# Zeroing both layers' gate arrays in the first mixer, with a fourth activation buffer and a third kept group

## The chip, the core and the metric

One core of a Trainium2 chip runs the whole kernel. The metric is the device time of one execution in microseconds, the median of several runs. The engines named below are TensorE (PE, its weight loads PEld), VectorE (DVE), ScalarE (ACT), GpSimd (POOL) and SyncE (SP, which only issues transfers). SP, ACT and POOL each have a queue on which they issue DMA transfers.

## The reference

A decoder trunk of two layers on 512 tokens of width 1024, in float32. Each layer has a token mixer and a channel mixer, each followed by a layer norm of `alpha * h + sublayer(h)`.

```
for layer in range(2):
    mix = mixer_ab(h, ...) if layer == 0 else mixer_c(h, ...)
    h = layer_norm(alpha * h + mix)
    h = layer_norm(alpha * h + peer(h, ...))
```

The channel mixer (PEER) has 16384 experts. For each token, eight heads each find 16 experts by a two-part key search, with softmax weights called gates:

```
s_top, i_top = top_k(einsum('thpd,hpkd->thpk', q, sub_keys), 16)
cand = s_top[:, :, 0, :, None] + s_top[:, :, 1, None, :]
best, pos = top_k(cand.reshape(T, 8, 256), 16)
gate = softmax(best)
act = gelu(einsum('td,thkd->thk', x, u_tab[eid]))
out = einsum('thk,thkd->td', gate * act, v_tab[eid])
```

## The kernel before

The kernel treats the expert layer as dense matrix products for most tokens: the activations `gelu(x @ u^T)` of all 16384 experts are made, multiplied by a mostly empty array of gates and then by `v`. The experts come in 128 blocks of 128, four blocks to a group, 32 groups. Every fp32 operand is cut into a high part (a cast on ACT, line 173) and a low part (a subtraction on DVE, line 174), and each product is three matmuls (`mm3`, lines 189 to 191; `mm2`, line 1155).

The tokens are split three ways. Tokens 64 to 383 go the dense way entirely. The first 64 have their activations made by gathering rows of `u` (`urow`, line 752) and are then added to a gate array in DRAM, after which their `v` side is dense as well. The last 128 are gathered on both sides (`gather_rounds`, line 1001).

A layer passes through three stages.

- **Mixer.** `mixer_ab` in layer 0, `mixer_c` in layer 1, then the output projection and the norm. Weights stream in pieces of 512 KB through the five buffers of `raw` (`stream`) on SP's queue. In `mixer_ab` the four projections run in the order u (`pool_part`), q and k, v, g; `sums` (line 478 and after) works on u and is called after the q and k projection.
- **Routing.** `peer` opens a pool and makes a `Scatter` object. Its constructor creates the DRAM array `gz` of the layer (32 groups x 128 x 512 values, 8.4 MB), fills a tile with zeros on POOL (line 79) and writes it 32 times to DRAM, once for each group, on SP's queue (line 81). Then the key search runs, and beside it `lookahead` makes the activations of the first 24 groups (`NLA`): four blocks at a time into a tile `ge`, of which there are three. A finished tile is spilled to DRAM (`sp`, line 775) unless its group is one of the last two (`KEEP`), which stay on chip. The gathered activations of the first 64 tokens are added into `gz` by indirect transfers on POOL (line 131). The gates of the other dense tokens are built on chip and stored to a second DRAM array, `gd` (line 947); for the three groups that come first afterwards they are also copied into tiles (`self.first`).
- **Experts.** `experts` walks over all 32 groups in the list `order`: one fresh group (number 27), the kept ones, then the fresh ones spread evenly among the spilled. For each group `fetch` gets the activations (a spilled group is loaded again on ACT's queue, line 1060; a fresh one is computed) and the gates: `gd` (line 1066) and `gz` (line 142), on ACT's queue after the first few, into one of three `gt` tiles. `high` and `low` multiply and split (lines 1100, 1104, 1111), `mm2` accumulates. Between the blocks, `gather_rounds` handles the last 128 tokens.

The program text gives dependencies, not the order of issue: the framework arranges each engine's instructions in advance, by a simulation in which an instruction can be issued as soon as it is ready. `issue_after` pins an instruction behind another on one engine. Within an engine's queue the order is then fixed.

The pool `sm` holds the small tiles of the norms (statistics, deviation and its reciprocal), four of each. Tiles called `gap` are never used; they take up space. The statistics of a block's first half (line 284) are taken as soon as the first half of the output projection is there.

Of the kernel before, what the change touches and what calls it, by code (L numbers as in the profile page):

```python
# [9 lines left out]
F32 = mybir.dt.float32  # L10
# [10 lines left out]
P = 128  # L21
# [8 lines left out]
NB = 4  # L30
NG = NE // NB
TD = 3 * P
NU = 64
TN = TD - NU
# [5 lines left out]
NSD = TD // 32  # L40
NLA = 24
NSZ = 4
KEEP = 2
ROT = 3
RAW = 5
QS = 8
# [16 lines left out]
class Scatter:  # L63


    def __init__(self, k, pool, layer):
        nc, self.tc = k.nc, k.tc
        self.name = "gz%d" % layer
        self.layer = layer
        self.head, self.last, self.now = -1, [], []  # L70
        self.todo = []
        self.rows = []
        self.gate = [k.pe.tile([P, 2, 16], F32, name="gate0", tag="gate0", bufs=4) for _ in range(4)]
        self.idx = [k.pe.tile([P, 2 * 16], I32, name="idx0", tag="idx0", bufs=4) for _ in range(4)]
        self.pcol = pool.tile([P, 1], F32, name="pcol", tag="pcol")
        nc.sync.dma_start(out=self.pcol, in_=k.io["pcol"])
        self.dst = k.dram.tile([NG, P, NSZ, NB, 32], F32, name=self.name, tag=self.name)
        z = pool.tile([P, NSZ * NB * 32], F32, name="zero", tag="zero")
        nc.gpsimd.memset(z, 0.0)
        for g in range(NG):  # L80
            nc.sync.dma_start(out=self.dst[g].rearrange("p s b t -> p (s b t)"), in_=z)

    def place(self, k, pool, c, k0, k1):
        nc = k.nc
# [62 lines left out]
class Kern:  # L147
    def __init__(self, ctx, tc, io):
        self.tc = tc
        self.nc = tc.nc  # L150
        self.io = io
        self.dmaq = 0
        E = ctx.enter_context
        self.const = E(tc.tile_pool(name="const", bufs=1))
        self.big = E(tc.tile_pool(name="big", bufs=1))
        self.st = E(tc.tile_pool(name="st", bufs=6))
        self.raw = E(tc.tile_pool(name="raw", bufs=RAW))
        self.sm = E(tc.tile_pool(name="sm", bufs=4))
        self.dram = E(tc.tile_pool(name="dram", bufs=1, space=DRAM))
        self.psA = E(tc.tile_pool(name="psA", bufs=2, space=PSUM))  # L160
        self.psB = E(tc.tile_pool(name="psB", bufs=3, space=PSUM))
        self.psC = E(tc.tile_pool(name="psC", bufs=3, space=PSUM))
# [145 lines left out]
    def mixer_ab(self, xT, hs):  # L308
        nc, tc, io = self.nc, self.tc, self.io
        with tc.tile_pool(name="ab", bufs=1) as ab, tc.tile_pool(name="abk", bufs=1) as abk:  # L310
# [39 lines left out]
                    rot.extend([r1, r2])  # L350

            self.proj_T(w, 1, xT, sink_qk)
            for n in range(4):
                sums(n)
            q1, q2, k1, k2 = rot
            qd = []
            for i, q in enumerate((q1, q2)):
                t = ab.tile([P, T], F32, name="qd%d" % i, tag="qk%d" % i)
# [32 lines left out]
            for h in range(4):  # L391
                s = ab.tile([P, NTB, P], F32, name="sc%d" % h, tag="t%d" % h)
# [6 lines left out]
            for tb in range(NTB):  # L399
# [9 lines left out]
                if tb < NTB - 1:  # L409
                    new = []  # L410
                    for i in range(2):
# [3 lines left out]
                        if state is None:  # L415
                            s = ab.tile([P, 512], F32, name="state%d" % i, tag="state%d" % i)
                            nc.vector.tensor_tensor(s, pk, bd, ALU.mult)
                        else:
                            s = state[i]
                            d = ab.tile([P, 512], F32, name="dst", tag="qk%d" % (2 + i))  # L420
# [14 lines left out]
            for tb in range(NTB):  # L435
                for h in range(4):
                    k = tb * 4 + h
# [3 lines left out]
            def turn(tb):  # L441
                self.transpose_in(o[:, tb].rearrange("p h e -> p (h e)"), xT, 4, 4, tb)
# [15 lines left out]
            self.proj_N(w, 3, xT, sink_g)  # L458
            turn(NTB - 1)
        return xT  # L460

    def pool_part(self, ab, xT, ya, w, icnt, pw, psc):
        nc = self.nc
# [231 lines left out]
    def peer(self, layer, xT, hs, out):  # L695
        nc, tc, io = self.nc, self.tc, self.io
        gd = self.dram.tile([NG, P, NSD - NSZ, NB, 32], F32, name="gd%d" % layer, tag="gd%d" % layer)
        sp = self.dram.tile([NLA, P, NB, TN], F32, name="sp%d" % layer, tag="sp%d" % layer)
        with tc.tile_pool(name="pe", bufs=1) as pe:
            self.pe = pe  # L700
            self.eid = pe.tile([P, P], I32, name="eid", tag="eid")
            self.gate3 = pe.tile([P, P], F32, name="gate3", tag="gate3")
            self.x3 = pe.tile([P, D], F32, name="x3", tag="x3")
            g, b = self.load_ln(layer, 0)

            def norm(tb):
                self.layernorm(tb, hs[tb], g, b, xT)
                if tb == NTB - 1:
                    nc.scalar.copy(self.x3, hs[tb])
                    nc.scalar.mul(hs[tb], hs[tb], ALPHA)  # L710

            self.out_proj(io["c_w_out" if layer else "ab_w_out"], xT, hs, norm)
            self.kept = {}
            self.urows = 0
            self.xx = pe.tile([P, D], F32, name="xx", tag="lng")
            for q in range(QN):
                nc.scalar.copy(self.xx[q * NU:(q + 1) * NU], hs[0][:NU])
            look = self.lookahead(layer, xT, sp)
            with tc.tile_pool(name="rk", bufs=1) as rk, ExitStack() as late:
                gz = Scatter(self, rk, layer)  # L720
                kT = rk.tile([P, (TD - P) // GW, 4, GW], F16, name="kT", tag="kT")
                iot = rk.tile([P, P, 2], F16, name="iot", tag="iot")
                nc.gpsimd.iota(iot, pattern=[[1, P], [0, 2]], base=0, channel_multiplier=0,
                               allow_small_or_imprecise_dtypes=True)
                credit = CREDIT0

                def routing():
                    yield from self.route_topk(layer, xT, kT, gz)
                    self.gx = late.enter_context(tc.tile_pool(name="gx", bufs=1))
                    self.first = {g: self.gx.tile([P, NSD, NB, 32], F32, name="gt", tag="gt", bufs=3)  # L730
                                  for g in (NLA + ROT, NLA - 2, NLA - 1)}
                    yield from self.route_gates(layer, kT, iot, gd)

                for cost in routing():
                    credit += cost
                    while credit >= 2.8:
                        credit -= 2.8
                        next(look, None)
                for _ in look:
                    pass  # L740
                g1, b1 = self.load_ln(layer, 1)
                self.experts(layer, xT, hs, gd, gz, sp, lambda tb: self.layernorm(
                    tb, hs[tb], g1, b1, None if layer else xT, out if layer else None))
        return xT
# [21 lines left out]

    def lookahead(self, layer, xT, sp):
        for g in range(NLA):
            ge = self.pe.tile([P, NB, TN], F32, name="ge", tag="ge", bufs=3)
            for b in range(NB):  # L770
                self.mm1(layer, g * NB + b, xT, ge[:, b, :], b % 2 == 1)
                if g >= NLA - KEEP:
                    self.kept[g] = ge
                elif b == NB - 1:
                    self.nc.sync.dma_start(out=sp[g], in_=ge)
                yield
# [252 lines left out]
    def experts(self, layer, xT, hs, gd, gz, sp, norm):  # L1029
        nc, tc, io = self.nc, self.tc, self.io  # L1030
        with tc.tile_pool(name="ex", bufs=2) as ex, tc.tile_pool(name="ga", bufs=2) as ga:
            ex.tile([P, 88], F32, name="gap", tag="gap", bufs=1)
            accs = [[(self.psC if hf else self.psB).tile([P, 512], F32, name="pC" if hf else "pB",
                                                          tag="pC" if hf else "pB") for hf in range(2)]
                    for _ in range(3)]
# [14 lines left out]
            def fetch(n):  # L1050
                if n >= NG:
                    return
                g = order[n]
                if g in kept:
                    ge = self.kept[g]
                else:
                    ge = self.pe.tile([P, NB, TN], F32, name="ge", tag="ge", bufs=3)
                q = nc.scalar if n > 1 else nc.sync
                if g < NLA and g not in kept:
                    q.dma_start(out=ge, in_=sp[g])  # L1060
                if g in self.first:
                    gt = self.first[g]
                    gz.read(nc.gpsimd, gt[:, :NSZ], g)
                else:
                    gt = self.gx.tile([P, NSD, NB, 32], F32, name="gt", tag="gt", bufs=3)
                    q.dma_start(out=gt[:, NSZ:], in_=gd[g])
                    gz.read(q, gt[:, :NSZ], g)
                ges[g] = (ge, gt)
# [49 lines left out]
            for i in range(NE):  # L1118
# [6 lines left out]
                g, b = order[i // NB], i % NB  # L1125
# [15 lines left out]
            for tb in range(3):  # L1141
                for hf in range(2):
                    for b in range(TAIL):
                        self.mm2(accs[tb], tb, cs[b - TAIL], vs[b - TAIL], False, b == TAIL - 1, (hf,))
                    z = hs[tb][:, hf * 512:(hf + 1) * 512]
# [21 lines left out]
    def run(self, out):  # L1167
        nc, io = self.nc, self.io
        self.epst = self.const.tile([P, 1], F32, name="epst", tag="epst")
        self.const.tile([P, 344], F32, name="gap", tag="gap")  # L1170
        nc.vector.memset(self.epst, EPS)
        hs = [self.big.tile([P, D], F32, name="h%d" % tb, tag="h%d" % tb) for tb in range(NTB)]
        xT = self.new_xT()
# [114 lines left out]
```

## Time and profile before

| | us |
|---|---|
| median of 3 runs | 2726.83 |
| lowest and highest | 2723.45, 2726.99 |
| profiled execution, its own time | 2726.43 |
| profiled execution, its span | 2724.6 |

The profile comes from one execution. Busy time is what each engine spent on its instructions; the transfers that an engine issues aren't counted in it. Matmuls overlap each other, so their busy times are an outline of when PE worked, and their number in a stretch tells its pace. "Idle before" is the time an engine stood before an instruction, with what released it; "issue" means that the profile shows nothing that it waited for.

By the timeline, layer 0 has its mixer to about 125 us, routing to about 655, experts to about 1305; layer 1 its mixer to about 1530, routing to about 2065, and experts to the end.

### The profile page before, as it was taken

How to read it: one execution, taken by the hardware profiler on the slowest of the kernel's cores; microseconds unless marked ns; L12 is line 12 of the kernel's file. 1: busy time of each engine (PE TensorE's matmuls, PEld its weight loads, DVE VectorE, ACT ScalarE, POOL GpSimd, SP SyncE). 2: the span in 40 equal slices, each digit the busy share in tenths (PEclk: the TensorE clock that was granted, in tenths of full speed). 3: DMA queues.
4: the chain of work that ended last, by engine and by line, in shares of the span. 5: the costliest groups of instructions: out<-in, count | busy, mean ns of one | idle time of the engine just before them, and what ended most of it. 6: DMA issues, size and time to landing. Idle time of an engine off the chain costs nothing.

```text
span 2724.6 us, 41889 instructions
## 1 busy us (share of the span) xinstructions
PE 2674.7 (98%) x15314; PEld 2374.7 (87%) x15314; DVE 2418.8 (89%) x4684; ACT 1101.2 (40%) x1587; POOL 1453.1 (53%) x931
## 2 busy tenths in 40 slices
PE   9999999999999999999999999999999999999998
PEld 7899999998888888887888899999998888887887
DVE  6679899997999999999798679999997999999999
ACT  3343334665333333333334354344664333333332
POOL 0005787786566556665000016777876566665653
PEclk9999999999999999999999999999999999999999
DMA  6357888799999999999322547889799999999995
GB/s 235 108 206 272 273 280 289 208 261 303 412 414 401 414 415 411 414 415 350 104 70 83 208 152 255 273 284 313 217 263 337 413 407 415 413 415 409 415 409 212
DMA packets 329423, 827.42 MB, mean 304 GB/s; under 512 B 63360, under 2 KB 129408, under 8 KB 329216
## 3 DMA queue, kind: packets, MB, share of 16 engines
q1 hardware_dynamic: 176672, 412.98, 42.6%
q0 software_dynamic: 129504, 337.31, 34.5%
q10 hardware_dynamic: 23040, 74.46, 6.8%
q8 instruction: 120, 1.97, 0.3%
q14 instruction: 87, 0.71, 0.1%
HBM read 743.23 MB, written 81.40 MB: 303 GB/s over the span
## 4 chain that ended last, share of the span: by engine, by line
PE 46%; DVE 15%; DMA 14%; issue 14%; POOL 10%; ACT 0%; DVEq 0%; POOLq 0%; SPq 0%; ACTq 0%
DMA row<-in_v,eid 10%; PE pA L191 7%; PE pA L189 7%; PE pA L190 7%; POOL row L1001 7%; PE pB L1155 7%; PE pC L1155 6%; DVE lo L174 3%; DMA urow<-in_u,ids 3%; DVE urow L109 2%; POOL gz L131 2%; PE pC L191 2%; PE pC L189 2%; PE pC L190 2%; DVE h L1026 2%
## 5 line engine op out<-in xcount | busy, mean ns | idle before, releaser
L173 ACT CAST hi<-raw 128x1024 fp32r<-128x1024 f32 (+1 forms) x609 | 636.5, 1050 | 858.9 <-PE pC L1155 152.5
L174 DVE TENSOR_TENSOR lo<-raw,hi 128x1024 fp32r<-128x1024 f32 (+1 forms) x609 | 728.7, 1213 | 65.7 <-ACT hi L173 62.6
L131 POOL DMA_INDIRECT gz<-gate,idx x256 | 513.2, 2005 | 138.4 <-issue 88.4
L1001 POOL DMA_INDIRECT row<-in_v,eid x256 | 404.6, 1581 | 335.8 <-DVE av L1013 263.5
L191 PE MATMUL pA<-xThi,lo 128*128 128x320 f32 (+2 forms) x1712 | 559.1, 327 | 6.4 <-DVE lo L174 6.4
L189 PE MATMUL pA<-xThi,hi 128*128 128x320 f32 (+2 forms) x1712 | 560.4, 327 | 0.8 <-ACT hi L173 0.8
L190 PE MATMUL pA<-xTlo,hi 128*128 128x320 f32 (+2 forms) x1712 | 558.2, 326 | 0.3 <-DVE xTlo L174 0.3
L1001 POOL DMA_INDIRECT row<-in_u,eid x256 | 361.4, 1412 | 135.6 <-issue 74.0
L1026 DVE SCALAR_TENSOR_TENSOR h<-row,cf,h 128x1024 f32<-128x1024 f32 x256 | 328.8, 1284 | 47.6 <-DMA row<-in_v,eid 46.8
L191 PEld LDWEIGHTS pA<-xThi,lo 128*128 128x128 f32 x1712 | 321.7, 188 | 23.2 <-DVE lo L174 8.8
L189 PEld LDWEIGHTS pA<-xThi,hi 128*128 128x128 f32 x1712 | 321.8, 188 | 17.4 <-ACT hi L173 2.0
L190 PEld LDWEIGHTS pA<-xTlo,hi 128*128 128x128 f32 x1712 | 321.7, 188 | 16.0 <-DVE xTlo L174 0.6
L1013 DVE CUSTOM_DVE_ANT_0 row<-row,x 128x1024 f32<-128x1024 f32 x256 | 310.8, 1216 | 27.3 <-DMA row<-in_u,eid 27.3
L1155 PE MATMUL pB<-lo,ch 128*128 128x512 f32 x768 | 302.6, 394 | 16.4 <-DVE lo L174 16.4
L1155 PE MATMUL pB<-hi,ch 128*128 128x512 f32 x768 | 302.2, 393 | 7.2 <-ACT ch L1104 7.2
L1155 PE MATMUL pB<-hi,cl 128*128 128x512 f32 x768 | 302.0, 393 | 0.5 <-DVE cl L1111 0.5
L1155 PE MATMUL pC<-lo,ch 128*128 128x512 f32 x768 | 301.7, 393 | 0.0
L1155 PE MATMUL pC<-hi,ch 128*128 128x512 f32 x768 | 301.7, 393 | 0.0
L1155 PE MATMUL pC<-hi,cl 128*128 128x512 f32 x768 | 301.5, 393 | 0.0
L752 POOL DMA_INDIRECT urow<-in_u,ids x128 | 162.4, 1269 | 243.4 <-ACT ids L92 181.4
L191 PE MATMUL pC<-xThi,lo 128*128 128x320 f32 x768 | 239.2, 311 | 5.5 <-DVE lo L174 5.5
L189 PE MATMUL pC<-xThi,hi 128*128 128x320 f32 x768 | 240.0, 312 | 0.3 <-ACT hi L173 0.3
(281 smaller groups left out, 4587.7 us busy)
## 6 DMA issues: line engine op xcount, KB each, us to landing
raw<-in_peer_ut SPq DMA_DIRECT2D x256, 512.0 KB, 5.8
raw<-in_peer_v SPq DMA_DIRECT2D x256, 512.0 KB, 8.5
gd<-gbuf SPq DMA_DIRECT2D x16, 2048.0 KB, 11.2
gt<-gd ACTq DMA_DIRECT2D x58, 512.0 KB, 7.8
sp<-ge SPq DMA_DIRECT2D x44, 640.0 KB, 6.6
ge<-sp ACTq DMA_DIRECT2D x44, 640.0 KB, 8.0
raw<-in_peer_w_q SPq DMA_DIRECT2D x32, 512.0 KB, 5.0
gz<-zero SPq DMA_DIRECT2D x64, 256.0 KB, 4.4
```

The source lines that it names most:

```text
L109: k.nc.vector.tensor_tensor_reduce(r, r, k.xx, 1.0, 0.0, ALU.mult, ALU.add, self.av[:, j:j + 1])
L131: d = nc.gpsimd.indirect_dma_start(out=flat, out_offset=bass.IndirectOffsetOnAxis(ap=self.idx[c][:, col], axis=0), in_=gate[:, col], in_of ...
L173: self.nc.scalar.copy(hi, src)
L174: return self.nc.vector.tensor_tensor(lo, src, hi.bitcast(F32), ALU.subtract)
L189: nc.tensor.matmul(ps, ah, bh, start=(first and i == 0), stop=False)
L190: nc.tensor.matmul(ps, ah, bl, start=False, stop=False)
L191: nc.tensor.matmul(ps, al, bh, start=False, stop=(last and i == n - 1))
L752: d = self.nc.gpsimd.indirect_dma_start(out=t, out_offset=None, in_=self.io["u%d" % layer], in_offset=bass.IndirectOffsetOnAxis(ap=ids[:, ...
L1001: nc.gpsimd.indirect_dma_start(out=t, out_offset=None, in_=io[name], in_offset=bass.IndirectOffsetOnAxis(ap=at, axis=0))
L1013: dot = nc.vector.tensor_tensor_reduce(ur, ur, x, 1.0, 0.0, ALU.mult, ALU.add, av[:, k:k + 1])
L1026: nc.vector.scalar_tensor_tensor(acc, vr, c, acc, ALU.mult, ALU.add)
L1155: nc.tensor.matmul(acc[hf], a[:, ts], b[:, hf * 512:(hf + 1) * 512], start=first and i == 0, stop=last and i == 2)
```

## The change

The gate arrays of both layers are created and zeroed in a new method, `zero_gates`, which `mixer_ab` calls after the q and k projection. It fills one tile with zeros on POOL and issues four transfers for each layer on ACT's queue, each covering eight groups (2 MB) by repeating the same tile. `Scatter` only takes the array of its layer.

`KEEP` becomes 3, and the tag `ge` has four buffers. The kept groups are 21, 22 and 23; the tiles prepared in `self.first` belong to groups 27, 21 and 22. In each layer 21 groups are spilled and loaded again instead of 22. The tile of zeros leaves the routing pool; `sm` has two buffers of each tile instead of four; two `gap` tiles become smaller.

```diff
-KEEP = 2
+KEEP = 3
...
-        self.dst = k.dram.tile([NG, P, NSZ, NB, 32], F32, name=self.name, tag=self.name)
-        z = pool.tile([P, NSZ * NB * 32], F32, name="zero", tag="zero")
-        nc.gpsimd.memset(z, 0.0)
-        for g in range(NG):
-            nc.sync.dma_start(out=self.dst[g].rearrange("p s b t -> p (s b t)"), in_=z)
+        self.dst = k.gz[layer]
...
-        self.sm = E(tc.tile_pool(name="sm", bufs=4))
+        self.sm = E(tc.tile_pool(name="sm", bufs=2))
...
             self.proj_T(w, 1, xT, sink_qk)
+            self.zero_gates(abk)
             for n in range(4):
                 sums(n)
...
+    def zero_gates(self, pool):
+        nc = self.nc
+        row = NSZ * NB * 32
+        z = pool.tile([P, row], F32, name="zero", tag="zero")
+        nc.gpsimd.memset(z, 0.0)
+        self.gz = []
+        for layer in range(2):
+            name = "gz%d" % layer
+            dst = self.dram.tile([NG, P, NSZ, NB, 32], F32, name=name, tag=name)
+            for g in range(0, NG, 8):
+                nc.scalar.dma_start(out=dst[g:g + 8].rearrange("g p s b t -> p g (s b t)"),
+                                    in_=z[:, None, :].broadcast_to([P, 8, row]))
+            self.gz.append(dst)
...
-                                  for g in (NLA + ROT, NLA - 2, NLA - 1)}
+                                  for g in (NLA + ROT, NLA - KEEP, NLA - KEEP + 1)}
...
-            ge = self.pe.tile([P, NB, TN], F32, name="ge", tag="ge", bufs=3)
+            ge = self.pe.tile([P, NB, TN], F32, name="ge", tag="ge", bufs=4)
...
-            ex.tile([P, 88], F32, name="gap", tag="gap", bufs=1)
+            ex.tile([P, 40], F32, name="gap", tag="gap", bufs=1)
...
-                    ge = self.pe.tile([P, NB, TN], F32, name="ge", tag="ge", bufs=3)
+                    ge = self.pe.tile([P, NB, TN], F32, name="ge", tag="ge", bufs=4)
...
-        self.const.tile([P, 344], F32, name="gap", tag="gap")
+        self.const.tile([P, 88], F32, name="gap", tag="gap")
```

## The prediction

> **What bounds the kernel now.** I read the page first, for the engines and the DMA row, then the busy time of each stage, then who waits for whom.
>
> ```profile
> span 2724.6 us, 41889 instructions
> PE 2674.7 (98%) x15314; PEld 2374.7 (87%) x15314; DVE 2418.8 (89%) x4684; ACT 1101.2 (40%) x1587; POOL 1453.1 (53%) x931
> ...
> GB/s 235 108 206 272 273 280 289 208 261 303 412 414 401 414 415 411 414 415 350 104 70 83 208 152 255 273 284 313 217 263 337 413 407 415 413 415 409 415 409 212
> ```
>
> PE is idle for only 49.9 us of 2724.6, so a change pays only where PE waits, and costs wherever it makes PE wait. The next view is the busy time by stretch: the columns are the stretch, its length, then busy time (instructions) of PE, PEld, DVE, ACT and POOL, the granted clock, the DMA share and GB/s.
>
> ```profile
> 0.00:25.00 25.00, 22.52 (x87) 15.83 (x88) 15.07 (x20) 14.28 (x15) 0.73 (x5) 1.00 0.87 300
> 0.00:50.00 50.00, 47.52 (x198) 36.54 (x199) 25.62 (x34) 22.94 (x27) 0.73 (x5) 1.00 0.77 278
> 50.00:120.00 70.00, 69.86 (x390) 55.36 (x389) 56.17 (x135) 24.48 (x37) 0.00 (x0) 1.00 0.19 65
> 125.00:215.00 90.00, 89.83 (x568) 82.66 (x567) 62.66 (x179) 39.12 (x53) 3.66 (x4) 1.00 0.62 212
> 1530.00:1650.00 120.00, 119.84 (x720) 108.51 (x719) 86.92 (x243) 45.45 (x63) 21.93 (x18) 1.00 0.68 245
> 215.00:655.00 440.00, 434.35 (x3096) 416.68 (x3095) 411.70 (x1205) 216.09 (x342) 335.12 (x191) 1.00 0.89 270
> 700.00:1310.00 610.00, 600.65 (x2860) 511.50 (x2860) 570.11 (x674) 212.27 (x256) 363.95 (x245) 0.99 0.99 395
> 2110.00:2725.00 615.00, 596.91 (x2840) 508.69 (x2838) 574.83 (x683) 207.01 (x250) 360.89 (x242) 0.99 0.97 390
> ```
>
> The first mixer (to about 125) starts DMA-heavy and then leaves the DMA engines nearly idle; PE runs through it. Where the zeroing stands today (125 to 215, 1530 to 1650) PE loses 0.17 and 0.16 us. Routing (215 to 655) runs PE and DVE together; the experts (from 700 and from 2110) run PE, DVE and DMA together.
>
> **The zeroing that goes.** SP issues 32 transfers of 256 KB in each layer:
>
> ```profile
> 125.05 23.79 SPq L81 DMA_DIRECT2D gz<-zero  x32
> ...
> 1533.67 22.81 SPq L81 DMA_DIRECT2D gz<-zero  x32
> ```
>
> That is 46.6 us of SP and 16.8 MB of writes, but beside them PE is busy 89.83 of 90 and 119.84 of 120 us with the output projection, whose weights were loaded before. What is late next is PE's own work. The gain lies between 0 and 0.33 us; I take 0. The POOL memset stands once instead of twice, on an engine that nothing waits for here.
>
> **The zeroing that comes.** Eight transfers of 2 MB (1024 rows of 2 KB) go out on ACT's queue, which also carries every cast of a weight and every copy out of PSUM. Two questions set the price: where they land in ACT's order, and how long they hold it.
>
> Where: the program's order is not the issue order. Each engine's instructions were arranged beforehand by when they become ready.
>
> ```profile
> 0.74 0.53 POOL L1162 MEMSET z<- 128x512 f16 x1 [0.29 <-POOLq L1278]
> ...
> 0.74 1.28 ACT L173 ACT_TABLE_LOAD   x1 [0.74 <-PEq L1278]
> 4.60 0.62 ACT L173 CAST xThi<-raw 128x512 fp32r<-128x512 f32 x1 [2.58 <-DMA raw<-in_xT]
> ...
> 5.95 0.07 DVE L478 MEMSET ws<- 128x16 f32 x1
> 6.01 0.69 DVE L174 TENSOR_TENSOR xTlo<-raw,xThi 128x512 fp32r<-128x512 f32 x1
> ...
> 46.96 1.06 ACT L173 CAST hi<-raw 128x1024 fp32r<-128x1024 f32 x1 [0.55 <-PE pA L190]
> ...
> 52.00 0.57 ACT L335 COPY qk<-pA 128x512 f32<-128x512 f32 x1
> ```
>
> The memset of line 478 belongs to `sums`, which the program reaches only after the second projection, just where the new call stands; it needs nothing, and it ran before the first subtraction. The casts at 46.96 belong after the copy at 52.00. The new transfers need only a POOL memset (0.53 us, POOL free from 1.27), so they are ready by about 2 us, while ACT waits until 4.60 for its first input. I expect them at the front of ACT's stream, in its first idle times, not at 52 us.
>
> How long: a transfer behind a large one is held until that one's rows have gone out.
>
> ```profile
> 654.73 0.38 SPq L947 DMA_DIRECT2D gd<-gbuf  x1
> 655.20 7.04 SPq L179 DMA_DIRECT2D raw<-in_peer_ut  x1
> ...
> 1048.19 0.95 DVE L1111 TENSOR_TENSOR cl<-gt,ch 128x768 fp32r<-128x768 f32 x1
> ...
> 1049.21 0.33 ACTq L1066 DMA_DIRECT2D gt<-gd  x1
> 1049.59 0.44 ACT L765 ACTIVATE ge<-pA 128x320 f32<-128x320 f32 x1 [8.44 <-issue]
> ```
>
> The 2 MB `gd` store takes 0.38 us itself, the small load behind it 7.04. And ACT stands still behind a transfer that can't go yet: until 1049.21 its fetch waited, and the activation behind it sat idle 8.44 us. By the zeroing rows one transfer of 2 MB takes 8 x 23.79 / 32 = 5.95 us; seven are held by the one before, 41.6 us in all. Three sizes follow. None of it covered: 41.6, if all eight go ahead of the first cast. All of ACT's idle time covers: ACT works 22.94 us in the first 50, and 22.94 + 41.6 = 64.6 needs 14.6 more. Between them, only the idle time of the start covers (25 - 14.28 = 10.7, while ACT waits for loads): 41.6 - 10.7 = 30.9. I take 30.9, because after 25 us ACT's idle time is time before PE's next result, and PE waits for that copy or for the next cast. Once PE has stood, its clock adds a little:
>
> ```profile
> 1294.24 2.72 PE pC L1155 x12
> ...
> 1230.00:1245.00 15.00, 13.21 (x46) 10.66 (x47) 15.00 (x18) 3.48 (x4) 8.60 (x6) 0.77 1.00 377
> ```
>
> A matmul comes every 2.72 / 12 = 0.227 us; after a stall, 46 of them took 13.21 instead of 10.4. One long stall adds 2.8 us, which I leave to the upper end: 41.6 + 2.8 = 44.4. The Trainium skill ("TensorE: Matmul & The Clock Gate", HAM oscillation) has PE fall to half clock after idle gaps of more than about 3.4 us. By that rule several stalls in the mixer would each pay again; the row, at a clock of 0.77 over 15 us, agrees in kind.
>
> **The kept group and the fourth buffer.** One spill and one reload fewer in each layer:
>
> ```profile
> sp<-ge SPq DMA_DIRECT2D x44, 640.0 KB, 6.6
> ge<-sp ACTq DMA_DIRECT2D x44, 640.0 KB, 8.0
> ```
>
> 44 become 42. The spill lies in routing, where PE and DVE set the pace: 0. The reload lies in the experts, at 413 GB/s: 0.655 MB / 413 = 1.6 us a layer if DMA sets the pace, 0 if PE does. Of 0 to 3.2 us I take 1.6. The fourth `ge` buffer relieves no wait that I find: ACT's fetch at 1049.21 waited for a `gt` buffer, which the subtraction begun at 1048.19 gave back at 1049.14, and `gt` keeps three. The order of the groups changes (three kept ones at the start, one old one fewer), and with it the places of such holds:
>
> ```profile
> PE pB L1155 <- DVE lo L174: 7.9, 2, 4.3
> ...
> PE pB L1155 <- DVE lo L174: 8.5, 2, 4.7
> ```
>
> These are PE's waits of the two expert stages, four in all, 16.4 us. I take no change, and keep 16.4 either way for the ends.
>
> **The small pool.** With two instead of four buffers, the early statistics of the third and fourth block (0.69 us each, at 136.03 and 143.39) move behind the first norm:
>
> ```profile
> 136.03 0.69 DVE L284 BATCH_NORM_STATS2 bst<-h 128x6 f32<-128x512 f32 x1
> 143.39 0.69 DVE L284 BATCH_NORM_STATS2 bst<-h 128x6 f32<-128x512 f32 x1
> ```
>
> DVE is busy 62.66 of 90 us there, so 0; with no cover 1.4 us in each of four norm passes, 5.5 in all. The `gap` tiles are padding: 0.
>
> **Sum.** The profiled execution took 2726.43 us, its span 2724.6; the median is 2726.83. 2726.4 + 30.9 - 1.6 = 2755.7, so 2756. Its own range is 2726.4 + 14.6 - 1.6 = 2739 to 2726.4 + 44.4 = 2771.
>
> **The rivals.**
>
> *Hidden zeroing, nothing else.* The eight transfers may be spread over ACT's idle time so that each finds the one before gone; ACT is idle for 45.5 us of the stretch 50 to 120, with DMA at 65 GB/s. Then only the reload is left: 2726.4 - 1.6 = 2725. For it speaks the idle ACT, against it the early readiness above.
>
> *Shared bandwidth only.* ACT isn't held, but the zeros share the start with the loads. 25 us at 300 GB/s are 7.5 MB; at half of the 413 GB/s of the experts' slices they take 36 us: up to 11 us late, 2736, and 2731 with half of it covered by the five `raw` buffers. The Trainium skill ("DMA: Bandwidth & Descriptors", Issuing engines are not separate DMA queues) says that transfers from SP, ACT and GpSimd run on the same 16 engines, and that another issuing engine saves only issue time, small beside the transfer; by that rule this rival is the whole effect. The zeroing rows don't bear out the small issue time: SP was held for all 23.79 us.
>
> *Faster.* The zeroing is hidden, and the new group order frees ACT of the fetch holds in the experts. It decides whether a `gt` buffer is back before ACT reaches its fetch. All four PE waits gone: 2726.4 - 16.4 - 1.6 = 2708; half of them, 2717. Against it: `gt` still has three buffers.
>
> *The change doesn't do what it says.* A kept group may save no time because PE paces the experts (600.65 of 610 us busy); that is the end of 0 taken above.
>
> **Chances.** Forecast 0.62; shared bandwidth 0.10 (0.08 of it beyond 5.5 us); hidden 0.18; faster 0.10. About 0.2%, or 5.5 us, is what a measurement of this kernel can tell from no change. So slower 0.70, same 0.20, faster 0.10. The range 2722 to 2770 holds nearly all of the forecast, the shared case and most of the hidden one, and leaves out the faster case and the far end of the hold.
>
> **What would show it.** In the profile after: the eight transfers on ACT's queue before 25 us, ACT idle behind them, and PE waiting for casts in the first 60 us, so that the first mixer ends about 31 us late; 125 to 215 shifted but not shorter; 42 spills and reloads; four or so PE waits of 4 us in the experts. I am wrong if the transfers stand after 50 us with ACT running on, or if the experts' stretch changes by more than a few microseconds.

## The result and the profile after

| | before | after |
|---|---|---|
| median | 2725.14 us (4 runs, 2720.64 to 2726.99) | 2752.71 us (4 runs, 2749.67 to 2756.17) |
| profiled execution, its own time | 2726.43 us | 2756.17 us |
| profiled execution, its span | 2724.6 us | 2754.4 us |

The ratio is 1.0105, with a 95% interval of 1.0092 to 1.0119: the change costs about 27.6 us. The line numbers of the kernel after differ a little: casts are on line 169 (173 before), streamed loads on 175 (179), the zero transfers on 469. The page of the kernel after, in the same parts as the page before:

```profile
span 2754.4 us, 41830 instructions
...
PE 2687.6 (98%) x15314; PEld 2380.9 (86%) x15314; DVE 2418.2 (88%) x4684; ACT 1102.0 (40%) x1587; POOL 1466.7 (53%) x930
...
PEclk8899999999999999999999999999999999999999
...
GB/s 379 129 111 237 252 282 285 228 241 286 387 406 415 408 415 408 415 414 384 110 92 62 115 106 273 277 277 306 205 270 318 407 407 414 410 414 404 415 403 208
```

The first of the 40 slices (68.9 us each) moved 379 GB/s where it moved 235, and the granted clock of the first two fell to 0.8. Later slices move less where the zeroing stood (slice 4: 237 for 272); the rest looks much as it did. The place of the loss is read from one instruction that stands at the end of the first mixer in both kernels, the load of `lng`. It is issued at 123.29 us before and at 150.82 after, 27.5 us late. At the second layer's mixer the same load is still 27.3 us late (1531.09 and 1558.36). So of the 29.8 us by which the two spans differ, 27.3 come from the first mixer; the other 2.5 are less than the spread of the runs above. The stretches behind it, moved by 28 us, in the busy-time view of the kernel after (stretch, length, then busy time and instructions of PE, PEld, DVE, ACT, POOL, the granted clock, DMA share and GB/s):

```profile
153.00:243.00 90.00, 89.85 (x570) 82.80 (x569) 62.66 (x180) 39.15 (x53) 3.07 (x2) 1.00 0.37 120
...
728.00:1338.00 610.00, 601.36 (x2877) 513.09 (x2876) 569.69 (x675) 214.01 (x259) 364.76 (x240) 0.99 0.98 393
1558.00:1678.00 120.00, 119.85 (x719) 108.63 (x718) 86.72 (x248) 46.38 (x63) 23.18 (x18) 1.00 0.50 176
```

PE is busy for 89.85 and 119.85 us where the zeroing left, against 89.83 and 119.84 before, although the DMA share fell from 0.62 to 0.37 and from 0.68 to 0.50. In the experts' stretch PE's busy time is the same to 0.7 us.

Within the first mixer the same view, up to the load of `lng`, splits the loss into two. First the kernel before:

```profile
0.00:123.29 123.29, 120.68 (x603) 94.62 (x604) 85.09 (x171) 47.52 (x64) 0.73 (x5) 1.00 0.44 156
```

Then the kernel after:

```profile
0.00:150.82 150.82, 136.81 (x603) 103.39 (x604) 84.49 (x171) 46.81 (x64) 1.19 (x6) 0.90 0.65 239
```

Both hold the same 603 matmuls. PE idled for 150.82 - 136.81 = 14.0 us instead of 2.6, which is 11.4 of the 27.5 us. The other 16.1 us are the same matmuls running longer (136.81 against 120.68): the granted clock was 0.90 on the mean, and a tenth of 150.82 is 15.1.

Where the eight transfers went, in the timeline of ACT of the kernel after (start, duration, engine, line, what; in brackets the idle time before and its releaser; ACTq is ACT issuing a transfer):

```profile
1.76 0.40 ACTq L469 DMA_DIRECT2D gz<-zero  x1
...
14.77 0.38 ACTq L469 DMA_DIRECT2D gz<-zero  x1
25.42 1.04 ACT L169 CAST hi<-raw 128x1024 fp32r<-128x1024 f32 x1 [9.61 <-DMA raw<-in_ab_w_in]
...
40.88 0.37 ACTq L469 DMA_DIRECT2D gz<-zero  x1
...
46.32 0.37 ACTq L469 DMA_DIRECT2D gz<-zero  x1
...
62.64 0.59 ACT L331 COPY qk<-pA 128x512 f32<-128x512 f32 x1 [4.85 <-PE pA L187]
62.64 2.97 ACTq L469 DMA_DIRECT2D gz<-zero  x2
65.71 4.83 ACT L169 CAST hi<-raw 128x1024 fp32r<-128x1024 f32 x5 [2.49 <-DVE r L342]
84.65 1.05 ACT L169 CAST hi<-raw 128x1024 fp32r<-128x1024 f32 x1 [14.11 <-DMA raw<-in_ab_w_in]
90.32 0.59 ACT L363 COPY v<-pA 128x512 f32<-128x512 f32 x1 [4.62 <-PE pA L187]
```

Two of the eight were issued before 25 us, the others were spread to 63.05 us, between instructions that wait for PE. Only the last pair held ACT for some time, 2.97 us. ACT's two longest waits were for weights: 9.61 us at 25.42, which made PE wait, and 14.11 us at 84.65. The second cost PE nothing: it is for a weight of the fourth projection, whose load went out only at 80.93, when its buffer came free, and PE was by then at work on `v`. SP, which loads those weights, stood still for the zeros, in the view of its waits up to 150 us (line waiting, what it waited for, us in total, times, longest):

```profile
SPq L175 <- DMA gz<-zero: 19.5, 3, 11.9
SPq L325 <- DMA gz<-zero: 8.5, 1, 8.5
```

And the transfers as such, in the page's list of DMA issues (KB each, median us from issue to landing):

```profile
sp<-ge SPq DMA_DIRECT2D x42, 640.0 KB, 6.6
ge<-sp ACTq DMA_DIRECT2D x42, 640.0 KB, 8.4
gz<-zero ACTq DMA_DIRECT2D x8, 2048.0 KB, 16.6
```

A transfer of 2 MB took 16.6 us to land (the median of the eight).

The loss grows in two steps. The last copy of q and k starts at 52.00 us before and at 62.64 after: 10.6 us late. In the kernel before, `v` follows at once. Its weights are cast from 46.96 to 51.04, ahead of that copy, its first product starts at 51.07, and its first block is copied at 56.71:

```profile
56.71 0.59 ACT L366 COPY v<-pA 128x512 f32<-128x512 f32 x1 [4.13 <-PE pA L191]
```

In the kernel after, `v`'s first block is copied only at 90.32 (above). Its casts stand behind the last pair of zero transfers in ACT's order, and the subtractions stand behind most of `sums` in DVE's order. PE has transposes and three of the four pool products ahead of `v`, for which it waits for DVE. First a line of DVE's timeline, then two of PE's:

```profile
79.69 1.22 DVE L170 TENSOR_TENSOR lo<-raw,hi 128x1024 fp32r<-128x1024 f32 x1
...
79.09 2.08 PE L497 MATMUL pB<-pp,pw 128*128 128x512 f32 x2 [1.86 <-DVE pp L495]
80.18 1.84 PE L185 MATMUL pA<-hi,xThi 128*128 128x512 f32 x2
```

The other 16.9 us arise here, before `v` starts at 80.18, and no wait of PE for a transfer stands in this step. Of `v`'s four weights three landed at 41.30, 43.26 and 53.90 us; for the other one, issued at 33.84, the trace gives no landing. So the framework's order is another one than before. Why it chose this one, and what the old order would have given, no run shows.

The transfers spilled and reloaded went from 44 to 42, as the change says.

### The profile page after: what moved, and what is told of

Its sections match the earlier page's. It is cut to its first block, busy times and chain, and to the rows that moved or that the text cites. A ratio compares the mean times of both kernels' runs of the same rounds, so it can differ in the third digit from the quotient of the medians.

```text
span 2754.4 us, 41830 instructions
## 1 busy us (share of the span) xinstructions
PE 2687.6 (98%) x15314; PEld 2380.9 (86%) x15314; DVE 2418.2 (88%) x4684; ACT 1102.0 (40%) x1587; POOL 1466.7 (53%) x930
## 4 chain that ended last, share of the span: by engine, by line
PE 51%; DVE 14%; issue 12%; DMA 11%; POOL 11%; ACT 0%; SPq 0%; DVEq 0%; POOLq 0%; ACTq 0%
PE pB L1166 10%; PE pC L1166 10%; PE pA L187 7%; PE pA L185 7%; PE pA L186 7%; POOL row L1012 6%; POOL gz L127 4%; DMA row<-in_v,eid 4%; DVE lo L170 3%; DMA urow<-in_u,ids 3%; DMA row<-in_u,eid 2%; DVE urow L105 2%; PE pC L187 2%; PE pC L185 2%; PE pC L186 2%
## 5 line engine op out<-in xcount | busy, mean ns | idle before, releaser
L1012 POOL DMA_INDIRECT row<-in_v,eid x256 | 418.9, 1636 | 324.1 <-DVE av L1024 245.2
L186 PEld LDWEIGHTS pA<-xTlo,hi 128*128 128x128 f32 x1712 | 322.8, 189 | 16.1 <-DVE xTlo L170 0.4
L1166 PE MATMUL pB<-lo,ch 128*128 128x512 f32 x768 | 302.6, 394 | 18.2 <-DVE lo L170 18.2
## 6 DMA issues: line engine op xcount, KB each, us to landing
gz<-zero ACTq DMA_DIRECT2D x8, 2048.0 KB, 16.6
```

Source lines behind the costliest of these rows:

```text
L186: nc.tensor.matmul(ps, ah, bl, start=False, stop=False)
L1012: nc.gpsimd.indirect_dma_start(out=t, out_offset=None, in_=io[name], in_offset=bass.IndirectOffsetOnAxis(ap=at, axis=0))
L1166: nc.tensor.matmul(acc[hf], a[:, ts], b[:, hf * 512:(hf + 1) * 512], start=first and i == 0, stop=last and i == 2)
```

## The experiments

Four readings were open. **A, bandwidth:** for its first 40 us the first mixer has hardly any DMA bandwidth to give, and 16.8 MB beside the weight loads push these back. **B, the prediction's own:** ACT is held while it issues large transfers, and its casts and copies come late. **C:** another part of the change costs (the kept group, the buffers). **D:** SP's loads wait for the landing of zero transfers issued before them, so the long landings are the harm. The letters were given anew after the first runs: in the first two expectations quoted below, A is the hold of ACT, and B (B1 and B2) the waiting and the sharing of SP's loads. A fifth reading, that the new order of instructions is part of the harm, has no run of its own. All kernels below are the kernel after with the edit shown.

### The zeros late, still on ACT

The eight transfers are pinned behind ACT's last copy of `v`, where the DMA engines have little to do (A sees no cost) and ACT has copies to make (B sees one).

```diff
-            self.zero_gates(abk)
...
-                nc.scalar.copy(v[:, tb, :], ps)
+                self.vcopy = nc.scalar.copy(v[:, tb, :], ps).ins
...
             self.proj_N(w, 2, xT, sink_v)
+            with tc.issue_after(self.vcopy):
+                self.zero_gates(abk)
```

> The changed kernel with one difference: the eight transfers of zeros are pinned on ACT's queue behind the last copy of v (76.8 us in the kernel before), where the DMA engines moved 65 GB/s. Theory A, as predicted (ACT is held about 5.95 us behind each transfer of 2 MB): the holds of up to 41.6 us now lie between the v copies and the output projection, where ACT still has casts and copies of the mixer to do, so much of the loss stays: about 2735 to 2750 us. Theory B (SP's own loads wait until a transfer of zeros has landed, and share the DMA engines with them at the start): no load is due soon at that place, so nearly all of the 27 us goes: 2722 to 2728 us.

Measured: 2736.54 us (2734.76 to 2740.97), against 2724.01 for the kernel before on the same chip; ratio 1.0046 (1.003 to 1.0063). ACT's timeline in this kernel:

```profile
76.61 35.24 ACTq L470 DMA_DIRECT2D gz<-zero  x8
111.89 1.56 ACT L406 COPY o<-pB 128x512 f32<-128x512 f32 x3 [34.70 <-issue]
```

And its busy time by stretch:

```profile
90.00:100.00 10.00, 10.00 (x56) 8.62 (x55) 2.08 (x3) 0.00 (x0) 0.00 (x0) 1.00 1.05 405
100.00:110.00 10.00, 3.07 (x14) 2.22 (x12) 0.00 (x0) 0.00 (x0) 0.00 (x0) 0.86 1.04 397
110.00:120.00 10.00, 7.47 (x35) 7.06 (x36) 7.07 (x38) 7.85 (x13) 0.00 (x0) 0.63 1.03 385
```

The hold exists: eight transfers back to back keep ACT for 35.24 us, and the copy behind them waits 34.70. But PE had some 25 us of work that needs no ACT, so it waited for ACT's copies only for 9.46 us, to 112.53. `lng` came at 134.70, 11.4 us late. So B's mechanism is real, and here costs a third of the hold. In the kernel after the transfers weren't back to back, and no hold there was longer than the 2.97 us.

### The zeros early, on POOL's queue

The same bytes at the same point of the program, from an engine with no work in this stage, as 64 transfers of 256 KB.

```diff
-            for g in range(0, NG, 8):
-                nc.scalar.dma_start(out=dst[g:g + 8].rearrange("g p s b t -> p g (s b t)"),
-                                    in_=z[:, None, :].broadcast_to([P, 8, row]))
+            for g in range(NG):
+                nc.gpsimd.dma_start(out=dst[g].rearrange("p s b t -> p (s b t)"), in_=z)
```

> The changed kernel with the zeros issued on POOL's queue at the same early place, as 64 transfers of 256 KB. The bytes and their time are about the same; ACT isn't held, and SP no longer counts them among its own transfers. Theory A (ACT held): the loss goes, 2722 to 2730 us. Theory B1 (SP's loads wait for the landing of a transfer of zeros, whatever the bandwidth): the loss goes as well, 2722 to 2730 us. Theory B2 (the zeros take bandwidth from the loads of the first 40 us): the bytes are still there, and 10 us or more of the 27 stay: 2735 us or more.

Measured: 2749.58 us (2743.42 to 2754.98), ratio 1.01 (1.0083 to 1.0117). ACT issues no zeros here, and no wait of SP for a zero transfer is left. The first mixer still ends 24.5 us late, with `lng` at 147.83. Its busy time up to there, and the worst stretch within:

```profile
0.00:147.83 147.83, 127.81 (x603) 98.81 (x604) 85.10 (x171) 46.76 (x64) 35.89 (x70) 0.93 0.63 244
...
50.00:60.00 10.00, 3.41 (x8) 2.73 (x9) 5.14 (x7) 3.06 (x4) 4.18 (x8) 0.50 1.03 419
```

And the longest of ACT's waits up to 100 us:

```profile
ACT hi L169 <- DMA raw<-in_ab_w_in: 32.1, 10, 16.3
```

The casts wait for weights, and the weights for DMA engines whose share is 1.03 at 419 GB/s. Here PE idles for 20.0 us (147.83 - 127.81), 17.4 more than before, and its slower matmuls add 7.1: another split, nearly the same sum. The first weight of `v` goes out at 40.00 us and lands at 52.60; before it went out at 25.94. PE's order of work is that of the kernel before here: `v` follows q and k at once, at 69.23 (51.07 before), with the pool products in between and the transposes behind. So late weights alone, without B, without D and without another order, are enough for a loss of nearly this size.

### Only the zeroing moved, and only the group kept

The first of these keeps `KEEP` at 2 and three `ge` buffers.

```diff
-KEEP = 3
+KEEP = 2
...
-            ge = self.pe.tile([P, NB, TN], F32, name="ge", tag="ge", bufs=4)
+            ge = self.pe.tile([P, NB, TN], F32, name="ge", tag="ge", bufs=3)
```

> The zeroing moved as in the change, but two kept groups and three ge buffers as before. If the whole loss comes from the moved zeroing: 2750 to 2756 us, and the first mixer ends as late as in the changed kernel (its norm weights loaded at about 151 us instead of 123). If the kept group or its order of the groups costs or gains something, this differs from the changed kernel by that: the prediction's 1.6 us gain would put it at about 2754.

Measured: 2748.39 us (2747.45 to 2751.1), ratio 1.0091 (1.0075 to 1.0108); `lng` at 149.16, 25.9 us late. The time is a little below the expected 2750 to 2756 us; against 2724.01 for the kernel before on that chip it is a loss of 24.4 us, with an interval that overlaps that of the kernel after.

```profile
0.00:149.16 149.16, 133.91 (x603) 100.91 (x604) 84.48 (x171) 46.83 (x64) 1.19 (x6) 0.92 0.66 242
```

The moved zeroing is the loss, as far as these intervals tell; PE's order is that of the kernel after, and `v` starts at 79.37. The second kernel has the third kept group, the fourth buffer and the small pool, and zeroes each layer's array at the start of `peer` as the kernel before did, from memory that is free there.

```diff
-            self.zero_gates(abk)
...
             g, b = self.load_ln(layer, 0)
+            self.gz = self.dram.tile([NG, P, NSZ, NB, 32], F32, name="gz%d" % layer, tag="gz%d" % layer)
+            z = self.x3[:, :NSZ * NB * 32]
+            nc.gpsimd.memset(z, 0.0)
+            for n in range(NG):
+                nc.sync.dma_start(out=self.gz[n].rearrange("p s b t -> p (s b t)"), in_=z)
```

> Three kept groups, four ge buffers and the small pool as in the change, but each layer's zeros are written where they were before, on SP's queue at the start of peer, from the space of x3, which is not filled until later. The prediction's terms: the reload saves 0 to 3.2 us and nothing else moves: 2722 to 2726 us. If the new order of the groups removes ACT's holds in the experts: down to 2708. If it adds holds: up to 2735.

Measured: 2725.24 us (2720.23 to 2729.2, 10 runs) against 2724.01, ratio 1.0002 (0.9993 to 1.0012). C falls, and the kept group brings nothing that can be measured. The interval excludes a gain of more than 1.9 us, but not the forecast 1.6.

### The zeros late, on SP

Now the bytes go where bandwidth is free, and from a queue with little to do: 256 KB pieces on SP, pinned behind the last load of the fourth projection's weights. In the first kernel everything else is as after; the second has two kept groups and three `ge` buffers, so that it is the move of the zeroing alone.

```diff
-        nc.sync.dma_start(out=raw, in_=src)
+        self.fed = nc.sync.dma_start(out=raw, in_=src).ins
...
-            self.zero_gates(abk)
...
             self.proj_N(w, 3, xT, sink_g)
+            with tc.issue_after(self.fed):
+                self.zero_gates(abk)
...
+            for g in range(NG):
+                nc.sync.dma_start(out=dst[g].rearrange("p s b t -> p (s b t)"), in_=z)
```

> The changed kernel, with the same 16.8 MB of zeros as 64 transfers of 256 KB from SP's queue, behind the last load of the first mixer's last projection. SP and the DMA engines have little to do there. Theory A (the first mixer's opening has no DMA bandwidth to give away; zeros beside the weight loads push them back): the whole loss goes, 2722 to 2727 us, and the load of lng is issued at 123 us plus or minus 2. Theory B (ACT is held by issuing): the same, since ACT issues none. Theory C (something else of the change costs, such as the kept groups or the buffers): the loss stays, 2745 or more. If removing the zeroing from the peer's start were worth something by itself, the time would come below 2722.

> Late zeros from SP's queue as in the first of these runs, but with two kept groups and three buffers of activations as in the kernel before: the move of the zeroing alone, where it costs no bandwidth. By the prediction's step that the zeroing removed from the peer's start is worth nothing: 2723 to 2726 us, ratio 0.9995 to 1.0005. If it is worth something: below 2722.

Measured: 2725.17 us (2723.17 to 2729.62, 12 runs) with everything, ratio 1.0005 (0.9996 to 1.0013); 2722.97 us (2719.9 to 2731.08, 12 runs) for the move alone, ratio 0.9996 (0.9985 to 1.0006). The kernel before took 2725.44 on this chip. In the first of the two:

```profile
0.00:123.41 123.41, 120.90 (x602) 94.40 (x603) 84.95 (x171) 47.27 (x64) 1.19 (x6) 1.00 0.81 292
...
50.00:120.00 70.00, 70.00 (x391) 55.42 (x390) 56.36 (x134) 24.57 (x37) 0.00 (x0) 1.00 0.84 304
```

The stretch from 50 to 120 us, at a DMA share of 0.19 before, now carries the zeros at 0.84, and PE is busy for all 70 us. `lng` is issued at 123.41. The whole loss is gone with the place of the bytes. Neither kernel is measurably faster than the one before.

### Small pieces on ACT, and half the bytes

The first kernel leaves the zeros early on ACT but in 256 KB pieces (`nc.scalar` in place of `nc.gpsimd` in the diff for POOL above), meant to shorten the landings that SP waits for. The second puts only layer 0's zeros early on POOL, and layer 1's late on SP.

```diff
+            if layer:
+                continue
+            for g in range(NG):
+                nc.gpsimd.dma_start(out=dst[g].rearrange("p s b t -> p (s b t)"), in_=z)
...
             self.proj_N(w, 3, xT, sink_g)
+            with tc.issue_after(self.fed):
+                for g in range(NG):
+                    nc.sync.dma_start(out=self.gz[1][g].rearrange("p s b t -> p (s b t)"), in_=self.z)
```

> The changed kernel, its zeros as early and on ACT's queue as before, but as 64 transfers of 256 KB instead of 8 of 2 MB. Theory A (bandwidth): the bytes are the same, 2743 to 2756 us. Theory D (SP's loads wait for the landing of a zero transfer of 16.6 us that was issued eight transfers earlier): landings get shorter, SP's waits for them fall from about 28 us to under 5, and most of the loss goes, 2730 or below. Theory B (ACT held by issuing): 64 issues hold ACT as long as or longer than 8, 2750 to 2775 us, and ACT's casts start late behind them with SP's loads landed.

> The changed kernel with the first layer's 8.4 MB of zeros early on POOL's queue and the second layer's late on SP's queue. Theory A (bandwidth): the loss goes with the bytes that stand beside the weight loads, about half of the 25.6 us that all of them early on POOL cost: 2734 to 2740 us, with lng issued at 133 to 138 us. If the opening had a slack of its own (DMA idle at 45 to 50 us before), less than half: 2728 to 2734. Theory D (landings of the 2 MB transfers): no such transfer here, 2722 to 2727.

Measured for the small pieces: 2755.76 us (2753.82 to 2757.18), ratio 1.0114 (1.0098 to 1.0131), `lng` at 154.99. SP's waits up to 150 us didn't shrink:

```profile
SPq L175 <- DMA gz<-zero: 29.7, 3, 25.5
SPq L367 <- DMA gz<-zero: 6.9, 3, 3.1
SPq L325 <- DMA gz<-zero: 4.9, 5, 1.7
```

And ACT's waits up to 100 us:

```profile
ACT qk L331 <- DMA gz<-zero: 26.1, 4, 8.9
ACT hi L169 <- DMA gz<-zero: 16.2, 1, 16.2
```

The longest of these, in ACT's timeline:

```profile
60.18 16.77 ACTq L469 DMA_DIRECT2D gz<-zero  x24
76.99 4.83 ACT L169 CAST hi<-raw 128x1024 fp32r<-128x1024 f32 x5 [16.25 <-DMA gz<-zero]
```

This run didn't do what it was made for: SP's waits for zeros grew to over 40 us, so it says nothing on D. It does say something on B: ACT stood for 26.1 + 16.2 = 42.3 us behind its own zeros. The last copy of q and k starts at 60.15, only 8.2 us late. Then 24 zero transfers stand in ACT's order ahead of `v`'s casts, and `v` starts at 84.00, 32.9 us late. So in this kernel the hold stood before `v`, as B has it. PE's order is again one with the transposes and all the pool products ahead of `v`. The time is only a few microseconds above that of the kernel on POOL's queue, where ACT stood behind no zeros (ratios 1.0114 and 1.01, with intervals that overlap). A and B both allowed the time measured, so it doesn't part them.

Measured for half the bytes: 2736.23 us (2732.06 to 2740.26), ratio 1.0042 (1.0027 to 1.0057), `lng` at 137.78:

```profile
0.00:137.78 137.78, 127.51 (x602) 98.56 (x603) 85.04 (x171) 46.93 (x64) 18.68 (x38) 0.95 0.70 262
```

The loss went from 25.6 us (2749.58 - 2724.01) to 10.8 (2736.23 - 2725.44): with half the bytes, a little under half the loss. That is A's range. (The profiled execution was the longest of the five, 2740.26, so its `lng` is later than the median suggests.) D, by which a kernel without 2 MB transfers would have no loss, falls as the whole explanation. What the runs show is that the early place of the bytes is the cause, and that sharing bandwidth is enough for a loss of this size. In the kernel with half the bytes, too, PE's order is that of the kernel before. The loss of the kernel after has about the same size, but not the same make-up. All three kernels that issue the zeros early on ACT's queue have the other order, with `v` behind the transposes and pool products; none of the others has it. In the first 10.6 us of the kernel after's loss, SP's stand of 8.5 us for a zero transfer comes just ahead of the loads for which ACT waited 9.61 us, and this isn't separated from bandwidth. In the other 16.9 us the order, ACT's hold of 2.97 us and the half clock aren't separated.

## Why the prediction was right in number and wrong in mechanism

The prediction was 2756.0 (2722 to 2770), the profiled execution took 2756.17 and the median is 2752.71. Step by step:

- **The zeroing that goes: 0.** Right. The stretches where it stood keep PE's busy time to 0.02 us, and the move alone, put where it harms nothing, gives a ratio of 0.9996 (0.9985 to 1.0006).
- **"I expect them at the front of ACT's stream, in its first idle times."** Half right. One transfer went ahead of the first cast, a second before 25 us. The other six were spread up to 63.05 us, three of them after 50 us, which the prediction named as a sign of being wrong. The `sums` memset on DVE showed that ready instructions can move ahead, not that all eight would move together.
- **"Seven are held by the one before, 41.6 us in all", less 10.7 of cover.** This is the step that failed as a mechanism. ACT was held for about 3 us in all. The hold exists where transfers go back to back: the late ACT run has 35.24 us for eight, where the sum says 41.6. In the kernel after, 10.6 us were lost by the end of the second projection, behind late weights, and 16.9 between it and the start of `v`, with another order of work. That the sum came out, 30.9 predicted and 27.5 measured at `lng`, is luck: neither part is in it. The term of 41.6 was worked out from the duration of such transfers, so it is close to the DMA time of the bytes (16.8 MB at 0.41 MB per us are 40.9 us). That makes it a bound for the sharing of bandwidth as well, which may be why it lies near. The cover of 10.7 us, ACT's idle time before 25 us, has no counterpart in the trace. Nor does ACT's queue carry every copy out of the tiles `pA`, `pB` and `pC`: DVE reads some of them itself (lines 488 and 393).
- **Clock: 2.8 us, left to the upper end.** Mis-sized. PE's busy time for the same matmuls grew by 16.1 us. The prediction allowed for one long stall; there were three episodes of half clock. In the third, PE also waited for DVE, so not all of the 16.1 us need be a loss by the clock.
- **The rival "shared bandwidth only".** Its mechanism is the one that the runs on POOL's queue bear out, and its chance of 0.10 was too low. Its price of 11 us is close to the 10.6 us lost by the end of the second projection, but it counted the first 25 us only, while the DMA engines were full for about 77. What it lacks is the later step, in which the order of work and the clock cost 16.9 us. By the rule quoted there from the Trainium skill ("DMA: Bandwidth & Descriptors", Issuing engines are not separate DMA queues), the issuing engine doesn't matter for the 16 shared engines; the trace agrees as to the sharing, with a DMA share of 1.03 at 419 GB/s beside POOL's zeros and 1.05 at 409 beside ACT's. That the losses are alike too, 24.5 us and 27.5, is in part chance, since the second holds another order of work. The same section calls the time of issuing usually small; in the late ACT run eight issues took 35.24 us.
- **The reload: -1.6.** Measured as nothing: ratio 1.0002 (0.9993 to 1.0012) for the kept group alone. The gain can't be told from the prediction's own end of 0, that PE paces the experts; 1.6 us isn't excluded. The experts' waits that could have moved by 16.4 us hardly did: that group is 18.2 us after, and with the next largest 27.8 against 23.6 before.
- **The small pool: 0.** Nothing speaks against it: the third block's statistics moved back as forecast, to 174.41 us, PE's busy time there stayed, and the kernel with late zeros on SP has it and is not measurably slower.
- **"Hidden zeroing", 2725.** It didn't happen in this change, but it is what the late zeros on SP do: 2725.17.

## What to carry to other kernels

Before work is moved to an "idle" queue, read the DMA share of the stretch where its bytes will travel, not the idle time of the engine that issues them: the same 16.8 MB cost about 25 us beside the first weight loads and nothing 50 us later. Their size over the bandwidth reached was a bound here that no run came up to. All the bytes are 40.9 us of it, and the early runs lost 24.5 to 31.7 at `lng`; half of the bytes are 20.5 us, and that run lost 10.8. Then look at the order of the instructions in the changed kernel: more than half of the loss in the kernel after arose while PE waited for no transfer. And a stage in which the tuned engine never waits gives nothing back when something beside it is removed.

## What the hardware showed

**Half clock comes after short gaps.** PE's timeline in the kernel after, around the three episodes:

```profile
7.39 0.49 PE L187 MATMUL pA<-xThi,lo 128*128 128x512 f32 x1
9.66 0.79 PE L185 MATMUL pA<-xThi,hi 128*128 128x512 f32 x1 [1.77 <-ACT hi L169]
...
22.60 0.39 PE L187 MATMUL pB<-xThi,lo 128*128 128x512 f32 x1
26.51 0.80 PE L185 MATMUL pA<-xThi,hi 128*128 128x512 f32 x1 [3.52 <-ACT hi L169]
...
65.25 0.63 PE L373 MATMUL pC<-c_ident,r 128*128 128x128 f32 x4 [2.65 <-issue]
67.26 1.12 PE L373 MATMUL pC<-c_ident,r 128*128 128x128 f32 x4 [1.38 <-DVE r L345]
```

And the granted clock (third column from the end) behind the third:

```profile
67.50:70.00 2.50, 2.50 (x20) 2.17 (x20) 1.95 (x5) 2.50 (x4) 0.00 (x0) 0.50 1.05 409
...
80.00:82.50 2.50, 2.50 (x6) 1.58 (x5) 2.20 (x4) 0.00 (x0) 0.00 (x0) 0.50 0.35 39
```

A matmul of 0.39 us took 0.79 after a gap of 1.77 us as it did after one of 3.52, and the third episode, after gaps of 2.65 and 1.38 us, lasted at least 15 us (clock 0.50 from 67.5 to 82.5), with PE not fully fed during it. The Trainium skill ("TensorE: Matmul & The Clock Gate", HAM oscillation) sets the gap that brings half clock at about 3.4 us. The trace agrees that each stall pays again; here gaps well below that length were followed by half clock too, with PE only partly busy around them.

**A load can wait for the landing of an unrelated transfer.** SP's own timeline in the kernel after:

```profile
16.36 0.33 SPq L325 DMA_DIRECT2D cos<-in_cos  x1
```

This is the load whose wait of 8.5 us for a zero transfer stands among SP's waits above. The first zero transfer was issued by ACT at 1.76 us and landed in 14.6 us, so at 16.36. `cos` shares no data with it; so one queue's long transfer can stop another queue's small loads. The instructions' records in the trace name the link: the zero transfer tells of its landing on semaphore 104, and the load of `cos` waits for that same semaphore and then uses it for its own landing. What a kernel with separate semaphores would gain was not tried.
